# Two model blocks on one core: the conditional overflow part as a loop over groups, splits between MoE and block 2 off GpSimd, and the shared expert's last layer in native fp32

## The chip, the cores and the metric

One core of a Trainium2 chip runs the whole program in one launch. The time is the device time in microseconds; three runs of the kernel before gave a median of 799.4 us (798.35 to 801.41). Engines: TensorE (PE; its weight loads are PEld), VectorE (DVE), ScalarE (ACT), GpSimd (POOL) and SyncE (SP), which here only issues DMAs. A "q" behind an engine's name (PEldq, DVEq) is its sequencer: waits, register work, branches.

## The reference, cut to what matters

256 tokens of width 1024 go through two blocks in fp32. The first has a mixer (attention and convolution) and a MoE; the second has pooling, windowed attention and a gated FFN. The MoE is where the change lies: 32 experts in 4 groups of 8; each token takes one group and two experts of it; beside them one shared expert sees all tokens.

```
g_w, g_idx = lax.top_k(g_prob, 1)                     # one group of 4 per token
e_w, e_idx = lax.top_k(e_prob, TOP_K)                 # two of its 8 experts
hid = jax.nn.silu(a) * b * combine[:, :, None]
routed = jnp.einsum('nef,efd->nd', hid, w_down)
shared = (jax.nn.silu(t @ w_sh_gate) * (t @ w_sh_up)) @ w_sh_down
x = h + rms_norm(routed + shared, post_ffn_norm)      # then the second block
```

## The kernel before

**Weights.** All weights come through one stream (class `Stream`): 167 chunks of 128 x 2048 fp32 (1 MB), each of two granules of 128 x 1024. SP loads chunks into a ring of 7 raw buffers (`RAWB`); a chunk's buffer is free, and the next load is issued, when its second granule has been split. `split` makes of a granule a high part (`whi`, a cast to fp32r on ScalarE, line 116) and a low part (`wlo`, a subtraction, line 119), on VectorE unless `eng`, `W.eng` or `alt` names GpSimd. Both parts have rings of 5 (`RING`). `take` hands out the next granule; `ahead(n)` splits up to n granules beyond the last one taken, `W.n` (4) when no n is given. A product of two such operands (`mm3`, lines 279 to 281) is three single-pass fp32r products: high x high, high x low, low x high.

**Whole granules.** `whole(n)` skips splitting for n chunks and hands out the raw fp32 data; `drop` then frees those chunks and loads the next. Chunks 14 and 15, the shared expert's first layer, are used so: `shared_first` (line 879) multiplies in native fp32.

**The MoE.** Tokens are gathered into one tile of 128 slots for each group by one-hot products. For each of 32 experts TensorE runs the first layer (`gu`), ScalarE and VectorE the gate (`expert_act`), then transposes (`expert_T`), and the last layer into `y`, one expert later. `group_end` splits a group's `y` into `yg`; `scatter` multiplies it by the group's one-hot `sel` and adds it to `ffn[i]`, the sum for token block i (two of 128 tokens). `shared_last` adds the shared expert's last layer to the same sums, from `sTh`/`sTl` (made by `shared_T` early in the MoE) and the granules 222 and 223, which stand in the stream ahead of the last expert's 224 and 225.

**The end of the MoE** (lines 1150 to 1232). `W.n` is set to 2 and `W.eng` to GpSimd. In order of the program: `shared_last(0, (0, 1))`; the last expert's last layer; `W.ahead()`; `group_end(3)`; the scatters of block 0, with one product of the shared layer for each half of block 1 in between (line 1163). Then `many`, the flag that a group has more than 128 tokens, is read into a register of every engine (line 1166), and `tc.If(many > 0)` (line 1167) holds the overflow part: for each of four groups, unrolled, products that gather further tokens, a device loop over 8 experts with their weights loaded anew, and products that add the result. Its products are plain fp32. Behind the `If`: `residual(0)` (norm, residual sum and the next norm's gain, on ScalarE and VectorE), the rest of block 1's sum, and the transposes `half_T` of block 0.

**The start of block 2** (lines 1291 to 1318). Block 0's transposed rows are split into `uTh`/`uTl`, four granules (226 to 229) taken, the queries of block 0 computed (`u_cols`), then `residual(1)`, its transposes, the queries of block 1, `rstd` and `diag` (`dg`, line 368) for both; `W.n` is back at 4, and `W.ahead()` splits 230 to 233, still on GpSimd. The product `spread` (`rs`) needs `dg`; then transposes of the queries (`q2T`), keys and values (`kv`), the pooling inputs (`zp`) and the scores.

**What sets the order.** The program is written against a planner that gives each engine its queue: it follows the order of the program by priority, but lets an instruction that is ready pass one that is not, by its own cost model. Each engine then works through its queue in order. An `If` is a unit: nothing of the outside is moved into it or across it. `tc.issue_after` puts an instruction behind a named one.

Of the kernel before, what the change touches and what calls it, by code (L numbers as in the profile page):

```python
# [11 lines left out]
F32 = mybir.dt.float32  # L12
F32R = mybir.dt.float32r
# [3 lines left out]
ALU = mybir.AluOpType  # L17
# [3 lines left out]
P = 128  # L21
D = 1024
NM = 16
S = 256
# [6 lines left out]
G = 1024  # L31

C_REP, C_MK0, C_MK1, C_LT, C_IOTA, C_REV, C_GB = 0, 128, 272, 544, 672, 1184, 1220
# [5 lines left out]
N_EXP = 32  # L39
CH_EXP = 16  # L40
# [13 lines left out]

ORDER = stream_order()


@with_exitstack
def block_kernel(ctx, tc, rwt, x, meta, pos, wst, gains, cst, pvec, rbias, sink, wpg, cst2, out):
    nc = tc.nc  # L60
    PE, ACT, DVE, POOL = nc.tensor, nc.scalar, nc.vector, nc.gpsimd
# [11 lines left out]
    def split(src, hi, lo, eng=None):  # L73
        ins = ACT.copy(hi, src)
        (eng or DVE).tensor_sub(lo, src, hi.bitcast(F32))
        return ins


    class Stream:
# [26 lines left out]
        def split(self, eng=None, part=None):  # L106

            g, low = self.s, None
            if g != G_HOLE:
                src = self.raw[g // 2][:, (g % 2) * G:(g % 2 + 1) * G]  # L110
                hi = wp.tile([P, G], F32R, name="whi", tag="whi", bufs=RING)
                lo = wp.tile([P, G], F32R, name="wlo", tag="wlo", bufs=RING)
                if self.alt and g % self.alt == 0:
                    eng = POOL
                eng = eng or self.eng or DVE
                ACT.copy(hi, src)  # L116

                def low():
                    eng.tensor_sub(lo, src, hi.bitcast(F32))  # L119

                if not part:
                    low()
                self.parts[g] = (hi, lo)
            self.s += 1
            if g % 2:
                del self.raw[g // 2]
                tag = self.place.get(g // 2)
                if not tag:
                    self.load()
                elif self.again[tag]:  # L130
                    self.again[tag] -= 1
                    self.load(tag)
            return low
# [29 lines left out]
            self.g += 1  # L163
            return self.parts.pop(self.g - 1)

        def whole(self, n):

            if self.s == G_HOLE:
                self.split()
            self.s0 = self.s  # L170
            self.g = self.s = self.s + 2 * n
            return [self.raw[self.g // 2 - n + c][:, a * G:(a + 1) * G] for c in range(n) for a in range(2)]

        def drop(self, n):
            for c in range(n):
                del self.raw[(self.s0 // 2) + c]
                self.load()

    W = Stream()
# [74 lines left out]
    def half_T(src, b, p=P):  # L254

        pt = mmt("tr")
        v = pt[:, :4 * p].rearrange("q (a t) -> q a t", a=4)
        for a in range(4):
            PE.transpose(v[:, a], src[:, (4 * b + a) * P:(4 * b + a + 1) * P], ident[:p, :p])
        return v  # L260
# [23 lines left out]
    def kb(w, k, n=P):  # L284
        return w[:, k * n:(k + 1) * n]
# [6 lines left out]
    def rows(o, w, ah, al, n, first, last):  # L292

        mm3(o, [(ah, al, kb(w[0], n, 512), kb(w[1], n, 512))], first=first, last=last)
# [571 lines left out]
    with tc.tile_pool(name="p2", bufs=1) as p2:  # L866
# [88 lines left out]
        DVE.tensor_scalar(ovf, most, float(P), None, op0=ALU.is_gt)  # L955


        ws = W.whole(2)
        gus = [shared_first(i, ws) for i in range(2)]
        W.drop(2)  # L960
        W.ahead()
        for tag in AGAIN:
            W.load(tag)
# [70 lines left out]
            return hh, hl  # L1034


        sTh = p2.tile([P, 2, S], F32R, name="sTh")
        sTl = p2.tile([P, 2, S], F32R, name="sTl")

        def shared_T(i, hs):  # L1040
            ht = mmt("hT")[:, :256]
            for f in range(2):
                PE.transpose(ht[:, f * P:(f + 1) * P], hs[:, f * P:(f + 1) * P], ident)
            ht = ht.rearrange("p (f t) -> p f t", f=2)
            split(ht, sTh[:, :, i * P:(i + 1) * P], sTl[:, :, i * P:(i + 1) * P])


        def slot_weights():
# [87 lines left out]
        def shared_last(i, ks):  # L1136
            for k in ks:
                for n in range(2):
                    rows(ffn[i][n], wsd[k], sTh[:, k, i * P:(i + 1) * P], sTl[:, k, i * P:(i + 1) * P],
                         n, k == 0, False)  # L1140

        def scatter(i, gs):
            for g in gs:
# [5 lines left out]

        g_pf = gain("post_ffn")  # L1150
        g_m2 = gain("mix2")
        W.n = 2
        W.eng = POOL
        wsd += [W.take(), W.take()]
        shared_last(0, (0, 1))
        last_cols(N_EXP - 1, hid)
# [2 lines left out]
        ffn[1] = [mmt("ffn10"), mmt("ffn11")]  # L1159
        group_end(3)  # L1160
        scatter(0, (0, 1, 2))
        for n in range(2):
            PE.matmul(ffn[1][n], sTh[:, 0, P:], kb(wsd[0][0], n, 512), start=True, stop=False, skip_group_check=True)
        scatter(0, (3,))

        many = nc.values_load(ovf[0:1, 0:1], min_val=0, max_val=1)
        with tc.If(many > 0):
            code2 = r3("code2")
            stt(code2, slot, -float(P) - 65536.0, over, ALU.add, ALU.add)
            ohx = p2.tile([P, 2, P], F32, name="ohx")  # L1170
            sx = p2.tile([P, S], F32, name="sx")
            cwx = p2.tile([P, 9], F32, name="cwx")
            sgx = p2.tile([P, S], F32, name="sgx", tag="sg", bufs=2)
            hx = p2.tile([P, S], F32, name="hx", tag="hs", bufs=2)
            hT = p2.tile([P, S], F32, name="hTx", tag="sg", bufs=2)
            xx, ya = w4("xx"), w4("ya")
            raw = p2.tile([P, 512], F32, name="rawx")
            pa, pb = acct("pa"), acct("pb")
            for g in range(4):
                for i in range(2):  # L1180
                    DVE.tensor_scalar(ohx[:, i], cs[:, C_IOTA + g * P:C_IOTA + (g + 1) * P],
                                      code2[:, i:i + 1], None, op0=ALU.is_equal)
                for b in range(2):
                    for a in range(4):
                        for i in range(2):
                            for src in (th, tl):
                                PE.matmul(kb(pa, a), kb(src[:, i], 4 * b + a).bitcast(F32), ohx[:, i],
                                          start=i == 0 and src is th, stop=i == 1 and src is tl,
                                          skip_group_check=True)
                    DVE.tensor_copy(kb(xx, b, 512), pa)  # L1190
                for i in range(2):
                    PE.matmul(pb[:, :9], ohx[:, i], comb[:, i, g], start=i == 0, stop=i == 1)
                DVE.tensor_copy(cwx, pb[:, :9])
                for i in range(2):
                    PE.transpose(kb(pb, i), ohx[:, i], ident)
                DVE.tensor_copy(sx, pb[:, :S])
                DVE.memset(ya, 0.0)
                with tc.For_i(0, 8, 1) as e:

                    def part(b):  # L1200
                        c = bass.ds(e * 3 + (CH_EXP + 24 * g + b // 4), 1)
                        nc.sync.dma_start(raw, wst[c, :, b % 4 * 512:b % 4 * 512 + 512].rearrange("o p f -> p (o f)"))

                    for k in range(8):
                        part(k)
                        PE.matmul(pa, kb(xx, k), raw, start=k == 0, stop=k == 7)
                    ACT.activation(sgx, pa[:, :256], AF.Silu, scale=cwx[:, 8:9])
                    stt(hx, pa[:, 256:], cwx[:, bass.ds(e, 1)], sgx)
                    for f in range(2):
                        PE.transpose(kb(pb, f), kb(hx, f), ident)  # L1210
                    DVE.tensor_copy(hT, pb[:, :256])
                    for k in range(2):
                        for n in range(2):
                            part(8 + 2 * k + n)
                            PE.matmul(pa, kb(hT, k), raw, start=True, stop=True)
                            DVE.tensor_add(kb(ya, n, 512), kb(ya, n, 512), pa)
                for i in range(2):
                    for n in range(2):
                        PE.matmul(pa, kb(sx, i), kb(ya, n, 512), start=True, stop=True)
                        DVE.tensor_copy(raw, pa)  # L1220
                        DVE.tensor_add(ffn[i][n], ffn[i][n], raw)
        s2 = sm(4)
        nx = [residual(0, ffn[0], g_pf, g_m2, s2)]
        for n in range(2):
            for a, w in ((sTh, wsd[0][1]), (sTl, wsd[0][0])):
                PE.matmul(ffn[1][n], a[:, 0, P:], kb(w, n, 512), start=False, stop=False, skip_group_check=True)
        scatter(1, (0, 2))
        shared_last(1, (1,))
        pts = [half_T(nx[0], 0)]
        scatter(1, (1,))  # L1230
        pts.append(half_T(nx[0], 1))
# [4 lines left out]
    with tc.tile_pool(name="p3", bufs=1) as p3:  # L1236
        uTh = p3.tile([P, 8, S], F32R, name="uTh", tag="th")
        uTl = p3.tile([P, 8, S], F32R, name="uTl", tag="tl")
        with tc.tile_pool(name="p3a", bufs=1) as q3:
# [63 lines left out]
            o_q.append(u_cols("q2", 1, ws, 512))  # L1303
            rn.append(rstd(s2[:, 2:4]))
            dgs.append(diag(rn[1], 0))
            W.n = RING - 1
            W.ahead()
            rs = acct("rs")[:, :S]
            spread(rs, dgs, [(0, P), (P, P)])
            DVE.tensor_copy(R, rs)  # L1310
            W.eng = None
            ws = [W.take() for _ in range(2)]
            for i in range(2):
                queries2(i, o_q[i])
# [487 lines left out]
```

## Time and profile before

| | |
|---|---|
| median of 3 runs | 799.4 us (798.35 to 801.41) |
| profiled execution, device time | 799.25 us |
| its span, first to last instruction | 797.5 us |
| mean granted clock of TensorE | 0.986 |
| busy: PE, DVE, ACT, POOL | 768.4, 613.8, 470.4, 65.1 us |
| DMA | 182.53 MB, mean 229 GB/s |

How to read the rows below. A timeline row gives start, duration (us), engine, line, operation, output<-inputs, shapes and count; in brackets the idle time ahead of it and what ended it. A row of waits gives who waited for whom: total us, times, longest. A row of a line's instructions gives shortest/median/longest duration in ns, then first and last start in us. A row of windows gives the stretch, its length, busy us and instructions of PE, PEld, DVE, ACT and POOL, the granted clock, the DMA share and GB/s. Matmul ends are modelled: each overlaps the start of the next, so the interval between starts is what a matmul costs.

### The profile page before, as it was taken

What the parts mean: (1) busy time and instruction counts of PE and PEld (TensorE: products, weight loads), DVE (VectorE), ACT (ScalarE), POOL (GpSimd) and SP (SyncE); (2) the same over time, 40 slices, a digit from 0 to 9 for tenths busy, and PEclk for the clock granted to TensorE, in tenths of its full rate; (3) what the DMA queues carried; (4) which work ended last, traced back from release to release, by engine and by line L of the source; (5) the groups of instructions that cost most, each with busy time, mean ns of one, the idle gap of its engine ahead of it and who ended that gap; (6) DMA issues with size and microseconds to landing.
All of it is one profiled execution on the core that took longest, in us unless ns stands there. A gap on an engine that the chain in (4) does not pass through costs nothing. (4 is left out here: it accounts for less than half of the span.)

```text
span 797.5 us, 11994 instructions
## 1 busy us (share of the span) xinstructions
PE 768.4 (96%) x4587; PEld 669.7 (84%) x4587; DVE 613.8 (77%) x983; ACT 470.4 (59%) x699; POOL 65.1 (8%) x70
## 2 busy tenths in 40 slices
PE   7989999999999999999999879999999999999996
PEld 5979985788888888888777668999988999999995
DVE  5878678899999989998986769856768566566565
ACT  4646445588788888887777345534556444444442
POOL 5631200000000000000003330000000000000000
PEclk9989999999999999999999999999999999999998
DMA  8736354699889979998998432445445455545101
GB/s 335 302 106 246 112 205 158 229 369 369 310 316 365 366 294 368 373 367 311 361 367 308 163 122 106 144 138 195 159 159 212 164 205 166 204 167 204 54 1 53
DMA packets 27217, 182.53 MB, mean 229 GB/s; under 512 B 3328, under 2 KB 3584, under 8 KB 6160
## 3 DMA queue, kind: packets, MB, share of 16 engines
q1 hardware_dynamic: 25344, 176.96, 59.8%
q0 software_dynamic: 1056, 3.71, 1.4%
q10 hardware_dynamic: 752, 1.01, 0.4%
q8 instruction: 38, 0.62, 0.3%
q14 instruction: 27, 0.22, 0.1%
HBM read 180.62 MB, written 1.05 MB: 228 GB/s over the span
## 5 line engine op out<-in xcount | busy, mean ns | idle before, releaser
L116 ACT CAST whi<-raw 128x1024 fp32r<-128x1024 f32 x328 | 339.8, 1049 | 186.6 <-PE gu L280 49.1
L119 DVE TENSOR_TENSOR wlo<-raw,whi 128x1024 fp32r<-128x1024 f32 x318 | 384.4, 1226 | 83.8 <-ACT whi L116 76.8
L279 PE MATMUL gu<-whi,xg 128*128 128x512 f32 x256 | 102.8, 401 | 0.0
L280 PE MATMUL gu<-wlo,xg 128*128 128x512 f32 x256 | 101.3, 396 | 0.0
L281 PE MATMUL gu<-whi,xg 128*128 128x512 f32 x256 | 100.7, 393 | 0.0
L280 PE MATMUL gu<-u2l,whi 128*128 128x256 f32 x320 | 90.6, 283 | 0.0
L279 PE MATMUL gu<-u2h,whi 128*128 128x256 f32 x320 | 90.6, 283 | 0.0
L281 PE MATMUL gu<-u2h,wlo 128*128 128x256 f32 x320 | 90.6, 283 | 0.0
L280 PEld LDWEIGHTS gu<-u2l,whi 128*128 128x128 f32 x320 | 61.5, 192 | 0.0
L281 PEld LDWEIGHTS gu<-u2h,wlo 128*128 128x128 f32 x320 | 61.4, 192 | 0.0
L279 PEld LDWEIGHTS gu<-u2h,whi 128*128 128x128 f32 x320 | 61.4, 192 | 0.0
L280 PEld LDWEIGHTS gu<-wlo,xg 128*128 128x128 f32 x256 | 48.2, 188 | 11.2 <-DVE wlo L119 1.4
L281 PEld LDWEIGHTS gu<-whi,xg 128*128 128x128 f32 x256 | 48.0, 188 | 10.5
L279 PEld LDWEIGHTS gu<-whi,xg 128*128 128x128 f32 x256 | 48.1, 188 | 9.9
L281 PE MATMUL y<-whi,hl 128*128 128x512 f32 x128 | 50.5, 394 | 0.0
L280 PE MATMUL y<-wlo,hh 128*128 128x512 f32 x128 | 50.5, 394 | 0.0
L119 POOL TENSOR_TENSOR wlo<-raw,whi 128x1024 fp32r<-128x1024 f32 x10 | 24.3, 2443 | 309.8 <-ACT whi L116 309.3
L279 PE MATMUL y<-whi,hh 128*128 128x512 f32 x128 | 48.7, 397 | 0.0
L279 PE MATMUL f<-whi,sh 128*128 128x512 f32 (+1 forms) x110 | 38.2, 349 | 0.0
L280 PE MATMUL f<-wlo,sh 128*128 128x512 f32 (+1 forms) x110 | 38.1, 349 | 0.0
L281 PE MATMUL f<-whi,sl 128*128 128x512 f32 (+1 forms) x110 | 37.8, 348 | 0.0
L279 PE MATMUL gt<-uTh,whi 128*128 128x256 f32 x128 | 36.7, 287 | 0.0
(468 smaller groups left out, 1529.8 us busy)
## 6 DMA issues: line engine op xcount, KB each, us to landing
raw<-in_wst_dram SPq DMA_DIRECT2D x164, 1024.0 KB, 4.8
gain<-in_gains_dram POOLq DMA_DIRECT2D x6, 512.0 KB, 4.3
raw<-in_wst_dram SPq DMA_DIRECT2D x5, 512.0 KB, 8.5
h<-in_x_dram SPq DMA_DIRECT2D x2, 512.0 KB, 4.8
cs<-in_cst_dram SPq DMA_DIRECT2D x1, 612.0 KB, 17.1
out_dram<-mg SPq DMA_DIRECT2D x2, 256.0 KB, 2.6
out_dram<-mg ACTq DMA_DIRECT2D x2, 256.0 KB, 2.8
c<-in_cst_dram POOLq DMA_DIRECT2D x1, 288.0 KB, 3.0
```

The source lines that it names most:

```text
L116: ACT.copy(hi, src)
L119: eng.tensor_sub(lo, src, hi.bitcast(F32))
L279: PE.matmul(o, sh, mh, start=first and i == 0, stop=False, skip_group_check=True)
L280: PE.matmul(o, sh, ml, start=False, stop=False, skip_group_check=True)
L281: last_mm[0] = PE.matmul(o, sl, mh, start=False, stop=last and i == n - 1, skip_group_check=True)
```

## The change

The chunk of the shared expert's last layer joins chunks 14 and 15 in a list `WHOLE`; `split` gives their granules out raw and leaves the buffer with the caller, who frees it by `drop(*chunks)`; `whole` goes. `shared_T` keeps one fp32 copy, and `shared_last` is one native fp32 product where it was three single-pass ones; block 1's first half of it now stands wholly ahead of the `If`, and the four products that completed it behind the `If` go. `W.n = 2` and `W.eng = POOL` go, with their resets. In the overflow part the four unrolled groups become a device loop around the loop over experts.

```diff
+WHOLE = [14, 15, ORDER.index(CH_EXP + 3 * N_EXP)]
...
         def split(self, eng=None, part=None):
             g, low = self.s, None
+            if g // 2 in WHOLE:
+                self.parts[g] = self.raw[g // 2][:, (g % 2) * G:(g % 2 + 1) * G]
+                self.s += 1
+                return low
...
-        def whole(self, n):
...
-        def drop(self, n):
-            for c in range(n):
-                del self.raw[(self.s0 // 2) + c]
+        def drop(self, *chunks):
+            for c in chunks:
+                del self.raw[c]
                 self.load()
...
-        ws = W.whole(2)
+        ws = [W.take() for _ in range(4)]
         gus = [shared_first(i, ws) for i in range(2)]
-        W.drop(2)
+        W.drop(*WHOLE[:2])
...
-            split(ht, sTh[:, :, i * P:(i + 1) * P], sTl[:, :, i * P:(i + 1) * P])
+            ACT.copy(sT[:, :, i * P:(i + 1) * P], ht.rearrange("p (f t) -> p f t", f=2))
...
         def shared_last(i, ks):
             for k in ks:
                 for n in range(2):
-                    rows(ffn[i][n], wsd[k], sTh[:, k, i * P:(i + 1) * P], sTl[:, k, i * P:(i + 1) * P],
-                         n, k == 0, False)
+                    PE.matmul(ffn[i][n], sT[:, k, i * P:(i + 1) * P], kb(wsd[k], n, 512), start=k == 0, stop=False,
+                              skip_group_check=True)
...
-        W.n = 2
-        W.eng = POOL
         wsd += [W.take(), W.take()]
...
-        for n in range(2):
-            PE.matmul(ffn[1][n], sTh[:, 0, P:], kb(wsd[0][0], n, 512), start=True, stop=False, skip_group_check=True)
+        shared_last(1, (0,))
         scatter(0, (3,))
...
-            for g in range(4):
+            with tc.For_i(0, 4, 1) as g:
                 for i in range(2):
...
+                DVE.tensor_scalar(code2, code2, -float(P), None, op0=ALU.add)
...
-                    PE.matmul(pb[:, :9], ohx[:, i], comb[:, i, g], start=i == 0, stop=i == 1)
+                    PE.matmul(pb[:, :9], ohx[:, i], comb[:, i, bass.ds(g, 1)].rearrange("p a b -> p (a b)"),
+                              start=i == 0, stop=i == 1)
...
         nx = [residual(0, ffn[0], g_pf, g_m2, s2)]
-        for n in range(2):
-            for a, w in ((sTh, wsd[0][1]), (sTl, wsd[0][0])):
-                PE.matmul(ffn[1][n], a[:, 0, P:], kb(w, n, 512), start=False, stop=False, skip_group_check=True)
         scatter(1, (0, 2))
         shared_last(1, (1,))
+        W.drop(WHOLE[2])
...
-            W.n = RING - 1
             W.ahead()
...
-            W.eng = None
```

## Rows read from the trace of the kernel before

**Rows 1.** Windows of 20 us from 440 to 500 us.
```profile
440.00:460.00 20.00, 17.88 (x78) 14.23 (x79) 16.01 (x45) 9.30 (x20) 7.76 (x7) 0.91 0.47 152
460.00:480.00 20.00, 15.22 (x100) 14.10 (x98) 13.43 (x14) 7.44 (x11) 7.24 (x7) 0.91 0.34 116
480.00:500.00 20.00, 18.21 (x145) 16.57 (x144) 19.65 (x58) 12.72 (x33) 0.28 (x4) 1.00 0.26 95
```
**Rows 2.** Waits from 425 to 470 us.
```profile
DVE mg L320 <- PEq L1167: 6.4, 1, 6.4
ACT whi L116 <- PE ffn L1226: 5.9, 1, 5.9
...
PE ffn L1226 <- PEq L1167: 4.8, 1, 4.8
PEld rs L374 <- DVE dg L368: 4.7, 1, 4.7
```
**Rows 3.** Instructions of line 1167, the `If`.
```profile
L1167 DVEq COMPARE_BRANCH  x1: 72/72/72, 435.4 to 435.4; - x1
...
L1167 DVEq EVENT_SEMAPHORE  x1: 21/21/21, 436.0 to 436.0; - x1
...
L1167 PEldq COMPARE_BRANCH  x1: 5152/5152/5152, 436.3 to 436.3; - x1
```
**Rows 4.** Timeline from 432 to 450 us: TensorE, ScalarE, VectorE.
```profile
433.42 2.24 PE L1146 MATMUL ffn<-yg,sel 128*128 128x512 f32 x9
...
435.74 1.09 PE L1146 MATMUL ffn<-yg,sel 128*128 128x512 f32 x4
...
437.61 0.20 ACT L205 ACTIVATION_READ_ACCUMULATOR junk<-ffn 128x1 f32 x1
...
442.27 0.15 DVE L248 SCALAR_TENSOR_TENSOR sm<-sm 128x1 f32<-128x1 f32 x1
...
443.74 0.75 DVE L252 SCALAR_TENSOR_TENSOR h<-mg,sm,h 128x512 f32<-128x512 f32 x1
444.52 0.69 DVE L339 TENSOR_TENSOR mg<-h,gain 128x512 f32<-128x512 f32 x1
...
449.89 0.49 PE L279 MATMUL q<-whi,uTh 128*128 128x512 f32 x1
```
**Rows 5.** Timeline from 444 to 468 us: GpSimd and VectorE.
```profile
444.83 2.65 POOL L119 TENSOR_TENSOR wlo<-raw,whi 128x1024 fp32r<-128x1024 f32 x1 [6.52 <-ACT whi L116]
...
445.85 2.18 DVE L252 SCALAR_TENSOR_TENSOR h<-mg,sm,h 128x512 f32<-128x512 f32 x1
...
457.55 0.28 DVE L368 TENSOR_SCALAR dg<-ident,sm 128x128 f32<-128x128 f32 x1
...
460.33 4.89 DVE L252 SCALAR_TENSOR_TENSOR sm<-sm,sm 128x1 f32<-128x1 f32 x3
460.49 7.02 POOL L119 TENSOR_TENSOR wlo<-raw,whi 128x1024 fp32r<-128x1024 f32 x3 [3.35 <-ACT whi L116]
...
465.25 2.42 DVE L368 TENSOR_SCALAR dg<-ident,sm 128x128 f32<-128x128 f32 x1
```
**Rows 6.** Instructions of line 119, the low parts, on VectorE.
```profile
L119 DVE TENSOR_TENSOR wlo<-raw,whi x318: 1205/1225/1795, 14.3 to 777.4; 128x1024 fp32r<-128x1024 f32 x159
```
**Rows 7.** Native fp32 products of `shared_first`: the line's instructions, and eight in the timeline.
```profile
L879 PE MATMUL gus<-raw,tT x32: 592/592/697, 122.6 to 143.5; 128*128 128x512 f32 x32
...
127.03 3.70 PE L879 MATMUL gus<-raw,tT 128*128 128x512 f32 x8 [0.29 <-ACT tT L862]
```
**Rows 8.** Windows behind the two holes of TensorE.
```profile
441.63:449.89 8.26, 8.26 (x34) 6.67 (x35) 7.47 (x15) 3.14 (x5) 3.99 (x2) 0.82 0.19 46
...
467.72:471.89 4.17, 3.91 (x19) 3.75 (x19) 2.56 (x4) 0.00 (x0) 0.00 (x0) 0.59 0.67 251
471.89:480.09 8.20, 8.20 (x68) 7.85 (x66) 3.38 (x5) 3.37 (x6) 0.14 (x2) 1.00 0.11 30
```
**Rows 9.** Timeline of VectorE at the end of the MoE.
```profile
434.02 1.29 DVE L75 TENSOR_TENSOR yg<-y,yg 128x512 fp32r<-128x512 f32 x2 [3.20 <-ACT yg L74]
```

More of the change, by code (lines that the diff above doesn't have):

```diff
@@ L164, in take @@
             return self.parts.pop(self.g - 1)
-        def whole(self, n):
[L168 to L172, printed above, removed]
-        def drop(self, n):
-            for c in range(n):
-                del self.raw[(self.s0 // 2) + c]
+        def drop(self, *chunks):
+            for c in chunks:
+                del self.raw[c]
                 self.load()
@@ L1034, in expert_T @@
             return hh, hl
-        sTh = p2.tile([P, 2, S], F32R, name="sTh")
-        sTl = p2.tile([P, 2, S], F32R, name="sTl")
+        sT = p2.tile([P, 2, S], F32, name="sT")
         def shared_T(i, hs):
@@ L1043, in shared_T @@
                 PE.transpose(ht[:, f * P:(f + 1) * P], hs[:, f * P:(f + 1) * P], ident)
-            ht = ht.rearrange("p (f t) -> p f t", f=2)
-            split(ht, sTh[:, :, i * P:(i + 1) * P], sTl[:, :, i * P:(i + 1) * P])
+            ACT.copy(sT[:, :, i * P:(i + 1) * P], ht.rearrange("p (f t) -> p f t", f=2))
         def slot_weights():
@@ L1178, in block_kernel @@
             pa, pb = acct("pa"), acct("pb")
-            for g in range(4):
+            with tc.For_i(0, 4, 1) as g:
                 for i in range(2):
-                    DVE.tensor_scalar(ohx[:, i], cs[:, C_IOTA + g * P:C_IOTA + (g + 1) * P],
-                                      code2[:, i:i + 1], None, op0=ALU.is_equal)
+                    DVE.tensor_scalar(ohx[:, i], cs[:, C_IOTA:C_IOTA + P], code2[:, i:i + 1], None,
+                                      op0=ALU.is_equal)
+                DVE.tensor_scalar(code2, code2, -float(P), None, op0=ALU.add)
                 for b in range(2):
@@ L1200, in part @@
                     def part(b):
-                        c = bass.ds(e * 3 + (CH_EXP + 24 * g + b // 4), 1)
+                        c = bass.ds(e * 3 + g * 24 + (CH_EXP + b // 4), 1)
                         nc.sync.dma_start(raw, wst[c, :, b % 4 * 512:b % 4 * 512 + 512].rearrange("o p f -> p (o f)"))
```

## The prediction

> **What bounds the kernel now.** I read the stretches of 20 us first. TensorE is busy nearly throughout, and the stretches around the conditional part are where it is not: 17.88, 15.22 and 18.21 of 20 us from 440 to 500 us, with a granted clock of 0.91 in two of them and VectorE at 19.65 in the third [rows 1]. So what happens between the MoE and block 2 is paid for at the end of the kernel; a microsecond gained there is kept as long as nothing later is waiting for another engine.
>
> The table of waits from 425 to 470 us names two holes of TensorE: 4.8 us behind line 1167 (the `If`), and 4.7 us in which `rs` waits for VectorE's `dg` [rows 2]. The events of line 1167 show what the first is: TensorE's compare-and-branch takes 5152 ns, VectorE's 72 ns, and VectorE is 0.6 us later at its next event (435.4 to 436.0) [rows 3]. VectorE's own idle time of 6.4 us ends on TensorE's event behind that branch [rows 2]; it is the same hole seen from the other engine. The overflow body is not executed: no row of its lines exists.
>
> The second hole is made by GpSimd. Three splits on it run from 460.49 for 7.02 us; in that time three [128 x 1] operations of VectorE take 4.89 us together and the 128 x 128 `dg` takes 2.42 us [rows 5]. I take the blocking as the cause because the same happens once more: `h<-mg,sm,h` takes 2.18 us beside the split of 444.83 and 0.75 us at 443.74, without one [rows 4, 5].
>
> **The change part by part.** The sum is made against the profiled execution: span 797.5, device time 799.25, which is 0.15 below the median of 799.4. E is the moment at which TensorE ends its work ahead of the `If`, now 435.74 + 1.09 = 436.83 [rows 4].
>
> *Native fp32.* Ahead of the `If`, 14 single-pass products go (12 of `shared_last(0)` and the two of line 1163) and 6 native ones come (4, and 2 of `shared_last(1, (0,))`). A single-pass product is issued every (2.24 - 1.09)/5 = 0.23 us, by the runs of nine and of four [rows 4]. A native one shows as two records (the 16 calls of line 879 have 32), 0.59 us long, which come every (3.70 - 0.59)/7 = 0.444 us, so 0.89 us a call [rows 7]. 6 x 0.89 - 14 x 0.23 = +2.1 us, all on the path, because TensorE has no gap there. So E moves to 438.9. Bounds: +1.9 (two records of 0.43) to +2.1. Two casts and two subtractions of the shared granules go as well: 2 x 1.22 us of VectorE [rows 6], ahead of time and worth nothing by themselves.
>
> *Four lookahead splits ahead of the `If` on VectorE.* Granules 226 to 229 are now split there, 4 x 1.22 = 4.9 us [rows 6]. Their cover: the 2.4 us just freed and the 3.20 us in which VectorE waits ahead of `yg` at 434.02 [rows 9]. They also no longer wait for ring slots, since 222 and 223 held two of the five until after the `If`. I take 0; without the cover the last split would sit ahead of `yg`: +1.2, still under the 2.76 us of twelve scatter products that TensorE has ahead of group 3's.
>
> *The branch.* By the code, TensorE's body is now four times 54 calls, 50 of them native with two records each: some 104 products and as many weight loads a group, over 800 instructions, and VectorE's four times 21 calls. Afterwards TensorE's is one group and two loops. VectorE's size of body costs 0.6 us, TensorE's 5.2 [rows 3]; the new one (over 208 instructions) lies between and much nearer to the small one. I take 0.6; bounds 0.1 and 5.2. TensorE's sequencer reaches the branch 0.53 us ahead of E (436.3), so 0.2 us of the 4.8 remain.
>
> [...]
>
> *What is late next.* The squares of the residual have run inside the hole: they end 0.98 us after E (437.81) [rows 4], and are now on the path. VectorE's chain then starts at 438.9 + 1.0 = 439.9 instead of 442.27, a shift of 2.4. It takes 3.58 us to the second `h` (442.27 to 445.85) [rows 4, 5], and that takes 0.75 us instead of 2.18, then 0.69 for the last `mg` (as at 444.52): done at 444.9. TensorE: from 439.1, eight scatter products 1.85, two native 1.8, to 442.8; four transposes 0.4 (their `mg` is done at 442.9), eight scatter products 1.85, transposes 0.4: 445.6, and there the queries start. They start at 449.89 now [rows 4]. [...]
>
> *No GpSimd behind the queries.* From 449.89 to the end of the queries nothing but the shift changes. Then `dg`, blocked, is the end of TensorE's wait. Unblocked, all of `rstd` takes 1.47 us (442.27 to 443.74 [rows 4]); its last three operations, which start at 460.33, and `dg` (0.28, as at 457.55 [rows 5]) then end by 461.4 on the old time axis, and TensorE waits from 467.72 - 4.7 = 463.0 on: the wait goes. Second term: **-4.7** [rows 2].
>
> *The clock behind that hole.* From 467.72 to 471.89 the granted clock is 0.59 and 19 products take 4.17 us; at 1.00, from 471.89, 68 take 8.20, 0.12 each [rows 8]. 19 x 0.12 = 2.3: third term **-1.9**.
>
> *The second four splits on VectorE (230 to 233).* 4.9 us, behind `dg` if the planner keeps the order of the program. From `dg` to the first scores VectorE would have some 12.1 us (457.1 to 469.2 on the new time axis) and needs the 2.56 + 3.38 that it does now [rows 8] + 4.9 = 10.8. That is cover with 1.3 us to spare. I count one split (1.2 us) as ending up ahead of a chain operation: **+1.2**; bounds 0 and 4.9.
>
> *Held buffer and the rest.* The raw buffer of the shared chunk is held until behind the `If`; DMA is at 0.34 from 460 to 480 [rows 1] and six buffers remain: 0. Body arithmetic (`code2`, dynamic slice) isn't executed: 0.
>
> Sum: -4.3 - 4.7 - 1.9 + 1.2 = -9.7; 799.25 - 9.7 + 0.15 = **789.7 us**.
>
> **Rivals.** (1) *The branch still waits for its code.* For it: the new body has still over twice the 84 calls of VectorE's. Against it: it is a quarter of the one that waits. Then TensorE restarts at 438.4 + 5.2 = 443.6, has 6.3 us of work to the queries and 1.6 us of slow clock more: 451.5, +1.6 instead of -4.3. 1.6 - 4.7 - 1.9 + 1.2 = -3.8: **795.6**.
>
> (2) *VectorE becomes the bound from the queries to the scores.* For it: 19.65 of 20 us from 480 [rows 1], and a cover of only 1.3. Against it: its blocked time, 8 us [rows 5], goes. All four later splits count: -10.9 + 4.9 = -6.0: **793.4**.
>
> (3) *A split stands in VectorE's queue ahead of a chain operation, its cast still waiting for a ring slot.* VectorE works in order, so `yg`, both residuals and `dg` are then as late as the slot; a cast waits up to 5.9 us for one now [rows 2], harmless while GpSimd takes the result. Price: all eight splits, 9.8, and one such wait, 5.9: -10.9 + 15.7 = +4.8, **804.2**. It decides from 10.9 us on. Against it: two ring slots come free, and a wait of that length needs a slot held across the `If`, which no granule does any more.
>
> **How the numbers follow.** Forecast 0.62 (786.7 to 792), rival 2 0.15, rival 1 0.15, rival 3 0.08. The low end is the sum without the +1.2, and with the 1.8 us that TensorE idles from 480 to 500 [rows 1] given back by an earlier VectorE: 786.7. The high end takes in rival 2 and rival 1, 796. A measurement here can tell about 0.5% from no change: faster is below 795.4, slower above 803.4. Faster: 0.62 + 0.15 + half of rival 1 = 0.84; same 0.09 (the other half, and what of rival 3 stays under 803.4); slower 0.07.
>
> **What would show it.** Right: TensorE's branch under 1 us and a gap there under 1 us; no operation of VectorE between 436 and 470 us beyond its usual length; `rs` right behind the queries; no stretch of low clock in either place; GpSimd without splits after the start. Wrong: a branch of 5 us again (rival 1); TensorE waiting for `wlo`, `qT` or `dg` from VectorE (rival 2); VectorE idle ahead of a split, on ACT's cast (rival 3).

## The result, and the profile after

The changed kernel takes 790.69 us (median of 4 runs, 789.21 to 791.99) beside 800.4 us of the kernel before: ratio 0.9873, 95% interval 0.9848 to 0.9899. The forecast was 789.7 us. Its profiled execution took 790.79 us with a span of 788.8.

Stretches of 20 us (length, busy time and instructions of PE, PEld, DVE, ACT and POOL, granted clock, DMA share, GB/s) answer [rows 1]:

```profile
440.00:460.00 20.00, 17.80 (x82) 13.83 (x83) 16.62 (x51) 9.59 (x23) 2.90 (x7) 1.00 0.51 181
460.00:480.00 20.00, 18.72 (x147) 17.09 (x146) 16.34 (x33) 8.49 (x13) 0.14 (x2) 1.00 0.58 211
480.00:500.00 20.00, 19.49 (x162) 18.80 (x159) 19.77 (x60) 15.75 (x45) 0.28 (x4) 1.00 0.15 54
```

The granted clock is 1.00 in all three, and TensorE's second stretch holds 147 products where it held 100. The events of the `If` (now line 1161) answer [rows 3]: TensorE's branch took 5152 ns and takes 353.

```profile
L1161 PEldq COMPARE_BRANCH  x1: 353/353/353, 436.6 to 436.6; - x1
...
L1161 PEldq EVENT_SEMAPHORE  x1: 51/51/51, 439.8 to 439.8; - x1
```

GpSimd is left with the two splits at the start of the program (instructions of line 125, the low parts):

```profile
L125 POOL TENSOR_TENSOR wlo<-raw,whi x2: 2355/2374/2394, 36.4 to 40.9; 128x1024 fp32r<-128x1024 f32 x2
```

TensorE's timeline after the change, which answers to that part of [rows 4]; the first row is the start of the last expert's transposes, `hT`, and the last one the first product of block 2's scores:

```profile
427.74 0.38 PE L1029 MATMUL hT<-ident,hs 128*128 128x128 f32 x2
...
441.84 1.88 PE L1136 MATMUL ffn<-raw,sT 128*128 128x512 f32 x4
443.15 2.20 PE L1143 MATMUL ffn<-yg,sel 128*128 128x512 f32 x7
445.19 0.60 PE L258 MATMUL tr<-ident,mg 128*128 128x128 f32 x4
445.54 0.48 PE L1143 MATMUL ffn<-yg,sel 128*128 128x512 f32 x1
447.88 0.63 PE L258 MATMUL tr<-ident,mg 128*128 128x128 f32 x4 [1.85 <-DVE mg L338]
448.26 0.48 PE L278 MATMUL q<-whi,uTh 128*128 128x512 f32 x1
...
460.98 0.38 PE L1274 MATMUL q2T<-ident,q2s 128*128 128x128 f32 x2
461.20 0.49 PE L373 MATMUL rs<-dg,ones 128*128 128x128 f32 x2
...
471.41 0.48 PE L1322 MATMUL s2a<-kT,qT 64*128 64x256 f32 x1
```

Of the two holes of [rows 2] nothing is left: `rs` stands behind the queries and two of their transposes without a wait. One wait of 1.85 us is new. I set the two executions against each other by three moments: `hT`, the first product of the queries, and the first product of block 2's scores, S. In the kernel before, the first and the last are these:

```profile
426.68 0.38 PE L1030 MATMUL hT<-ident,hs 128*128 128x128 f32 x2
...
480.10 0.48 PE L1330 MATMUL s2a<-kT,qT 64*128 64x256 f32 x1
```

| | hT | queries start | S | hT to queries | queries to S | hT to S |
|---|---|---|---|---|---|---|
| before | 426.68 | 449.89 | 480.10 | 23.21 | 30.21 | 53.42 |
| after | 427.74 | 448.26 | 471.41 | 20.52 | 23.15 | 43.67 |

So the change is worth 9.75 us between `hT` and S. From S to the end of the span nothing differs (797.5 - 480.10 = 317.40; 788.8 - 471.41 = 317.39). Ahead of `hT` the changed kernel's execution is 1.06 us late, and this is not the change. Three windows from 137.5 to 141.2 us, of before, of after, and of a later execution of the same changed kernel:

```profile
137.50:141.20 3.70, 3.70 (x17) 2.04 (x17) 2.79 (x13) 0.21 (x1) 0.00 (x0) 1.00 0.11 18
```
```profile
137.50:141.20 3.70, 3.70 (x7) 1.65 (x7) 2.78 (x13) 0.21 (x1) 0.00 (x0) 0.54 0.00 0
```
```profile
137.50:141.20 3.70, 3.70 (x15) 1.80 (x14) 3.26 (x19) 0.21 (x1) 0.00 (x0) 1.00 0.33 80
```

At a granted clock of 0.54, 7 records fit where 15 to 17 do at 1.00; ahead of it TensorE ran the same narrow products of `lg` without a pause in all three. In the later execution `hT` is at 425.62 instead of 427.74 and S at 469.30: the same 43.68 us between them, and a span of 786.7.

### The profile page after: what moved, and what is told of

Read it like the earlier page. It is cut to its first block, busy times and chain, and to the rows that moved or that the text cites. A ratio compares the mean times of both kernels' runs of the same rounds, so it can differ in the third digit from the quotient of the medians.

```text
span 788.8 us, 11966 instructions
## 1 busy us (share of the span) xinstructions
PE 766.5 (97%) x4579; PEld 665.4 (84%) x4579; DVE 611.8 (78%) x987; ACT 468.7 (59%) x697; POOL 45.7 (6%) x62
## 5 line engine op out<-in xcount | busy, mean ns | idle before, releaser
L125 DVE TENSOR_TENSOR wlo<-raw,whi 128x1024 fp32r<-128x1024 f32 x324 | 391.4, 1225 | 84.7 <-ACT whi L122 77.5
L280 PE MATMUL gt<-uTh,wlo 128*128 128x256 f32 x128 | 36.3, 283 | 0.0
```

What stands on the lines that cost most here:

```text
L280: last_mm[0] = PE.matmul(o, sl, mh, start=False, stop=last and i == n - 1, skip_group_check=True)
```

## The experiments

All ratios are to the kernel before, run beside each on the same chip (its median was 800.4 to 800.8). Stretches are from one profiled execution of each.

| run | median us | ratio, 95% interval | TensorE's branch | hT to queries | queries to S | hT to S |
|---|---|---|---|---|---|---|
| before | 800.7 | | 5.15 | 23.21 | 30.21 | 53.42 |
| after | 790.69 | 0.9873 (0.9848 to 0.9899) | 0.35 | 20.52 | 23.15 | 43.67 |
| e1, loop alone | 795.68 | 0.9951 (0.9934 to 0.9967) | 0.35 | 20.96 | 29.35 | 50.31 |
| e2, GpSimd alone | 798.12 | 0.9980 (0.9965 to 0.9995) | 5.77 | 27.38 | 24.44 | 51.82 |
| e3, native alone | 803.31 | 1.0027 (1.0009 to 1.0044) | 5.05 | 28.83 | 30.22 | 59.05 |
| e4, after unrolled | 798.34 | 0.9980 (0.9966 to 0.9995) | 6.11 | 29.07 | 23.21 | 52.28 |
| e5, loop and GpSimd | 789.83 | 0.9865 (0.9844 to 0.9886) | 0.35 | 20.09 | 24.71 | 44.80 |
| e6, two groups | 790.93 | 0.9873 (0.9849 to 0.9896) | 4.03 | 21.50 | 23.18 | 44.68 |
| e7, order | 788.78 | 0.9852 (0.9835 to 0.9870) | 0.35 | 19.46 | 23.99 | 43.45 |
| e8, GpSimd reads | 797.16 | 0.9952 (0.9933 to 0.9971) | 0.35 | 20.52 | 30.48 | 51.00 |

**Each part alone.** e1 is before with the loop over groups and nothing else:

```diff
-            for g in range(4):
+            with tc.For_i(0, 4, 1) as g:
...
```

> The kernel before with the loop over groups in the conditional part alone; GpSimd splits and three-product shared layer as before. Theory (two separate holes, each worth its own gap): TensorE's compare-and-branch falls from 5152 ns to about 0.4 us and its gap at the If from 4.8 to about 0.6 us; the queries of block 2 start 3 to 4 us earlier than at 449.89; the gap of 4.7 us ahead of rs and the low clock behind it stay. Time 3 to 4 us under the kernel before, ratio 0.995 to 0.997. Rival A (the gap at the If is the reading of the flag and the drain, not the size of the body): branch and time unchanged, ratio 1.000. Rival B (the gain of the change comes from the If alone, and the gap ahead of rs only moves with it): 8 to 10 us faster, ratio 0.988 to 0.990.

The first theory held: the branch is 0.35 us, the ratio lies in its range, and `rs` still waits, beside GpSimd's splits. The queries start 2.25 us earlier behind `hT`, less than the 3 to 4 expected, because TensorE now waits 1.98 us for `mg`. I take GpSimd's splits, which stay in e1, as the cause of this wait too. TensorE's timeline of e1:

```profile
442.58 0.63 PE L259 MATMUL tr<-ident,mg 128*128 128x128 f32 x4 [1.98 <-DVE mg L339]
...
464.18 0.80 PE L374 MATMUL rs<-dg,ones 128*128 128x128 f32 x2 [4.25 <-DVE dg L368]
```

e2 is before without the GpSimd splits, and so with a lookahead of 4 granules where it was 2:

```diff
-        W.n = 2
-        W.eng = POOL
...
-            W.n = RING - 1
...
-            W.eng = None
```

> The kernel before without GpSimd splits between MoE and block 2 alone (lookahead of 4 on VectorE); unrolled groups and three-product shared layer as before. Theory: no gap ahead of rs, no operation of VectorE beyond its usual length from 440 to 470 us, full clock in keys and values; branch still 5.1 us. Gain 4.7 + 1.9 less up to one split of 1.2: 5.4 to 6.6 us, ratio 0.992 to 0.993. Rival A (VectorE takes over 9.8 us of splits and becomes the bound): gain under 2 us, ratio 0.998 to 1.003, with TensorE waiting for wlo. Rival B (the gap ahead of rs is the wait for the squares, not GpSimd): the gap stays at over 3 us.

The direction was right and the size was not: 0.998 where more was expected. Behind the queries it gains 5.8 us, and ahead of them it loses 4.2. Of the loss 1.3 us are the first hole itself, 6.06 us behind a branch of 5.77 where it was 4.80 behind 5.15; why the branch is longer here no run shows. The other 2.9 lie between the hole and the queries. TensorE, ScalarE and VectorE in e2:

```profile
441.91 0.77 PE L1224 MATMUL ffn<-wlo,sTh 128*128 128x512 f32 x1 [6.06 <-PEq L1165]
```
```profile
443.99 1.04 ACT L116 CAST whi<-raw 128x1024 fp32r<-128x1024 f32 x1 [6.32 <-PE ffn L1224]
```
```profile
445.07 1.23 DVE L119 TENSOR_TENSOR wlo<-raw,whi 128x1024 fp32r<-128x1024 f32 x1 [1.28 <-ACT whi L116]
...
449.20 1.22 DVE L119 TENSOR_TENSOR wlo<-raw,whi 128x1024 fp32r<-128x1024 f32 x1 [0.72 <-ACT whi L116]
```

A cast waits 6.32 us until TensorE has read granules that hold their ring slots across the `If`, and its split stands in VectorE's order between the steps of `residual(0)`. A second one follows at 449.20. That is the third rival's mechanism, in a kernel in which slots are still held there; its price is 2.9 us and not the 15.7 that the rival gave it.

e3 is before with the native last layer alone:

```diff
-                    rows(ffn[i][n], wsd[k], sTh[:, k, i * P:(i + 1) * P], sTl[:, k, i * P:(i + 1) * P],
-                         n, k == 0, False)
+                    PE.matmul(ffn[i][n], sT[:, k, i * P:(i + 1) * P], kb(wsd[k], n, 512), start=k == 0, stop=False,
+                              skip_group_check=True)
...
```

> The kernel before with the shared expert's last layer in native fp32 from unsplit granules alone; GpSimd splits and unrolled groups as before. Theory: TensorE's work from the transposes of the last expert to the If grows by 1.5 to 2.1 us, behind the If four products fewer at the low clock give some of it back; both holes stay: 0 to 2 us slower, ratio 1.000 to 1.0025. Rival (freed ring slots and VectorE time make this edit a gain of its own): 2 us or more faster, ratio 0.9975 or less.

By the median it is 2.6 us slower, just beyond the theory's 2. But its profiled execution (804.45 us, where all twelve lie from 800.3 to 805.3) has 5.6 us more between `hT` and S. The native products account for 1.9 of it; the first hole is 6.74 us long instead of 4.80 (e4 below has the same), and the rest lies behind it, where the first eight products take 3.57 us and those in the kernel before 2.51 (at 443.47). Both holes stand in TensorE's timeline of e3:

```profile
445.01 3.57 PE L1143 MATMUL ffn<-yg,sel 128*128 128x512 f32 x8 [6.74 <-DVE mg L338]
...
472.42 0.80 PE L373 MATMUL rs<-dg,ones 128*128 128x128 f32 x2 [4.48 <-DVE dg L367]
```

**The changed kernel with one part taken back.** e4 unrolls the four groups again (the loop's edit reversed):

```diff
-            with tc.For_i(0, 4, 1) as g:
+            for g in range(4):
...
```

> The changed kernel with the four groups of the conditional part unrolled again. Theory: the branch is 5.1 us again and the gap at the If 4 to 5 us; the squares of the residual run inside it again, so the queries start 3 to 5 us later than in the changed kernel, and the rest follows; 3 to 5 us slower than the changed kernel, ratio to the kernel before 0.992 to 0.994. Rival (the loop matters little once GpSimd is gone, because VectorE's chain behind the If is the bound either way): within 1.5 us of the changed kernel, ratio 0.987 to 0.989.

The direction held, the size was double: 7.7 us over the changed kernel by the medians, 8.6 from `hT` to S. The branch and its event, then TensorE's weight loads (PEld) and products in e4:

```profile
L1161 PEldq COMPARE_BRANCH  x1: 6112/6112/6112, 434.5 to 434.5; - x1
L1161 PEldq EVENT_SEMAPHORE  x1: 51/51/51, 440.7 to 440.7; - x1
```
```profile
440.74 0.19 PEld L1143 LDWEIGHTS ffn<-yg,sel 128*128 128x128 f32 x1 [3.56 <-DVE wlo L125]
444.13 2.85 PEld L1143 LDWEIGHTS ffn<-yg,sel 128*128 128x128 f32 x7 [3.20 <-issue]
```
```profile
444.12 3.57 PE L1143 MATMUL ffn<-yg,sel 128*128 128x512 f32 x8 [6.51 <-DVE h L251]
```

One weight load comes right behind the event, and then there is none for 3.20 us, without a wait that the profile shows. The profile names `h` as the releaser, but `h` had ended 0.5 us before TensorE went on. Instruction fetches tell more: packets of 0.02 MB on DMA queue 8, which the profile lists as `instruction`, two from 436 to 445 us in each of before, e3, e4 and e6. The first one lands 1.4 to 1.5 us before the branch ends (in before at 440.04, the branch at 441.45). In e4 the second lands at 442.77, and TensorE goes on at 444.13, 1.36 us behind it. e3 shows the same: one load at 440.32, a fetch that lands at 443.60, the next load at 445.01, 1.41 us behind. So TensorE's second standstill in e3 and e4 ends like the branch, 1.4 us behind a fetch. In before (442.21 to 443.24) and e6 a second fetch came too, but TensorE had instructions in the meantime; why it had none in e3 and e4, no run shows. Then eight products take 3.57 us, at a granted clock of 0.50.

e5 takes the native products back and keeps loop and GpSimd edit, so it is before with the edits of e1 and e2.

> The kernel before with the loop over groups and without GpSimd splits; the shared expert's last layer as before, three products from split granules. Theory (native fp32 pays for itself because the raw granules leave two ring slots free; with them held across the If, the split of granule 229 stands in VectorE's queue ahead of the residual's chain and waits for its cast, as it did with the GpSimd splits alone removed): branch under 0.5 us, but one or two splits inside the chain of residual(0), so the queries start 2 to 4 us later behind the If than in the changed kernel; 1 to 3 us slower than the changed kernel, ratio to before 0.989 to 0.991. Rival (native fp32 only costs its 1.5 to 2.1 us of TensorE): faster than the changed kernel by 1.5 to 2 us, ratio 0.985.

This missed: the ratio lies under the theory's range, and no difference from the changed kernel can be told in the time. With the branch short, the ring slots come free at once: the cast that waited 6.32 us in e2 starts at 440.10 and waits for nothing (ScalarE in e5). Two splits still stand inside the chain of `residual(0)`, at 441.31 and 444.62, but they cost 1.22 us each and no wait, and TensorE saves the native products' 1.9 us.

```profile
440.10 1.05 ACT L116 CAST whi<-raw 128x1024 fp32r<-128x1024 f32 x1
```

From `hT` to S the profiled execution of e5 is even 1.13 us longer than the changed kernel's. It starts the queries 0.43 us earlier and loses 1.56 behind that, where the clock is low after a wait of 2.21 us for `mg` (window from the start of the queries):

```profile
448.23:452.00 3.77, 3.77 (x13) 2.97 (x12) 3.37 (x16) 0.73 (x3) 0.53 (x1) 0.57 0.73 238
```

So loop and GpSimd edit bring 0.49% and 0.20% alone and 1.35% together, and native fp32 adds nothing measurable to them. Each edit alone leaves a loss that the other takes away: in e1 TensorE still waits 1.98 us for `mg` and 4.25 for `dg`, in e2 the ring slots are still held for the length of the branch.

**How the branch depends on the body.** e6 is the changed kernel with two groups unrolled; groups 2 and 3 of the overflow part are left out (that part isn't executed here).

```diff
-            with tc.For_i(0, 4, 1) as g:
+            for g in range(2):
...
```

> The changed kernel with two groups unrolled in the conditional part instead of the loop over four; the overflow of groups 2 and 3 is left out (the part is not executed with these inputs). TensorE's body is then half of the unrolled one. Theory A (the cost is a step: code that lies beyond what has been fetched ahead costs a full fetch): branch of 5 to 6 us as with four groups, gap of 5 to 7 us, time as with four groups, ratio 0.996 to 0.999. Theory B (the cost grows with the size of the body): branch near 2.5 us, gap of 2 to 3 us, ratio 0.992 to 0.994. Theory C (two groups still lie within it): branch 0.35 us, time as the changed kernel, ratio 0.986 to 0.989.

None of the three came as a whole: the branch takes 4.03 us, nearest to A, but the kernel takes 790.93, the time of C. The branch begins at 437.6, 3.1 us ahead of the end of the products already queued, so TensorE idles only 1.11 us (event, then TensorE's timeline of e6):

```profile
L1161 PEldq COMPARE_BRANCH  x1: 4032/4032/4032, 437.6 to 437.6; - x1
```
```profile
441.83 2.10 PE L1143 MATMUL ffn<-yg,sel 128*128 128x512 f32 x8 [1.11 <-PEq L1161]
```

A body of half the length is neither free nor half the price: 0.35 us for one group's code, 4.03 for two, 5.05 to 6.11 for four. The four kernels with the same body differ by 1.06 us among themselves, so a single run at two groups doesn't show that the price grows with the length; it looks more like a step.

In before, e3, e4 and e6 the branches of 4.03 to 6.11 us end 1.4 to 1.5 us behind a fetch on queue 8. The one of 0.35 us in the changed kernel waits for none: no fetch on that queue lies between 428.46 and 438.44, and the branch ends at 436.99, so I take it that what it jumped to had been there already. Why it wasn't with two groups, no run shows.

**GpSimd and VectorE.** e8 adds three useless subtractions on GpSimd to the changed kernel, behind the second lookahead; they read what is there and write a tile that nobody reads:

```diff
+            jk = w4('jk')
+            for gg in (231, 232, 233):
+                POOL.tensor_sub(jk, W.parts[gg][0].bitcast(F32), W.parts[gg][0].bitcast(F32))
```

> The changed kernel with three useless subtractions on GpSimd added behind the second lookahead (from whi of granules 231 to 233 into a tile that nobody reads), nothing taken off VectorE. Theory (GpSimd's reads block VectorE): VectorE's operations ahead of dg or its splits take 2 us and more instead of 0.15 to 1.2; the wait of rs or of keys and values is 3 to 6 us again and the clock falls behind it; 4 to 7 us slower than the changed kernel, ratio 0.993 to 0.997. Rival (the gap of the kernel before was the planner's order of the splits, not the blocking): VectorE's durations as in the changed kernel, time within 1 us of it, ratio 0.986 to 0.989.

It came as expected, with operations of 1.8 to 1.9 us where I had 2 and more; the second hole is back, in full. GpSimd, VectorE and TensorE in e8:

```profile
456.27 7.69 POOL L1303 TENSOR_TENSOR jk<-whi 128x1024 f32<-128x1024 f32 x3 [3.42 <-ACT whi L122]
```
```profile
L1303 POOL TENSOR_TENSOR jk<-whi x3: 1890/2823/2824, 456.3 to 461.1; 128x1024 f32<-128x1024 f32 x3
```
```profile
456.11 2.06 DVE L251 SCALAR_TENSOR_TENSOR sm<-sm,sm 128x1 f32<-128x1 f32 x2
458.10 1.21 DVE L125 TENSOR_TENSOR wlo<-raw,whi 128x1024 fp32r<-128x1024 f32 x1
459.23 1.84 DVE L251 SCALAR_TENSOR_TENSOR sm<-sm,sm 128x1 f32<-128x1 f32 x1
461.00 1.21 DVE L125 TENSOR_TENSOR wlo<-raw,whi 128x1024 fp32r<-128x1024 f32 x1
462.13 1.91 DVE L367 TENSOR_SCALAR dg<-ident,sm 128x128 f32<-128x128 f32 x1
```
```profile
464.10 0.80 PE L373 MATMUL rs<-dg,ones 128*128 128x128 f32 x2 [4.78 <-DVE dg L367]
```

Nothing waits for the three subtractions, so it is their being there that makes VectorE's small operations long: a [128 x 1] one 1.84 us, and `dg` 1.91 instead of 0.28. VectorE's own splits stay at 1.21 us; beside each of them it is GpSimd's subtraction that grows, from 1.89 to 2.82, and the small operation behind the split ends within 0.1 us of that subtraction (`dg` at 464.04, the last subtraction at 463.96).

**The new wait.** e7 is the changed kernel with `uTl(0)` and `residual(1)` put behind the last `mg` of `residual(0)` in VectorE's order:

```diff
+            mg0 = last[1].ins
+            with tc.issue_after(mg0):
+                transpose_split(nx[0], uTh, uTl, P, 0, pts=pts)
-            transpose_split(nx[0], uTh, uTl, P, 0, pts=pts)
```

> The changed kernel with VectorE's order mended behind the If: the low part uTl of token block 0 and the whole of residual(1) stand behind the last mg of residual(0). In the changed kernel TensorE waits 1.85 us for that mg, because VectorE has uTl ahead of it, and uTl waits for ScalarE. Theory: that wait shrinks to under 0.5 us, the queries start about 1.5 us earlier behind the If, and all of it stays: 1 to 2 us under the changed kernel, ratio to before 0.985 to 0.986. Rival (the queries of block 1 and residual(1) are the bound and absorb it): within 0.5 us of the changed kernel, ratio 0.987 to 0.988.

The wait of 1.85 us goes and the queries start 1.06 us earlier behind `hT`, but by S only 0.2 us of it is left. To see whether the order is worth anything I ran the changed kernel and e7's again on one chip, in five rounds, and with them e5 with e7's order:

> The changed kernel again, in five rounds beside the next two on one chip. Both theories: 790 to 791 us, ratio to before 0.987; the queries start 20 to 21 us behind the last hT and TensorE waits some 1.9 us for VectorE's mg ahead of them.

> The changed kernel with uTl(0) and residual(1) behind the last mg of residual(0) in VectorE's order. Theory L (the 1.85 us in which TensorE waits for mg is what the first term lacked, and a microsecond gained there is kept): 1.0 to 1.5 us under the changed kernel, about 789.3, ratio of the two 0.9985 or less with an interval that leaves out 1. Rival (the wait only changes its place, 0.59 and 0.66 us showing instead, and the stretch is 0.2 us shorter): no difference that five rounds can tell.

> Before with the loop, without the GpSimd splits and with the same order of VectorE, but the shared expert's last layer in three single-pass products. Theory N (native fp32 costs TensorE 1.5 us ahead of the If and saves VectorE about as much behind it; with VectorE's order mended its saving is smaller, its cost the same): 0.5 to 1.5 us under the run with native fp32 and the mended order. Rival (the two keep cancelling): the same time within 0.1%.

The changed kernel took 788.78 us, 0.9864 (0.9836 to 0.9892); with the new order 790.41, 0.9870 (0.9847 to 0.9893); with the new order and single-pass products 790.37, 0.9866 (0.9840 to 0.9893). No order of the three can be told; an interval of a quarter of a per cent leaves out neither the 1 us of theory L nor the 0.5 of theory N. The stretches speak for the rivals: from `hT` to S the changed kernel takes 43.68 us, the new order 43.43, the new order with single-pass products 43.00. The wait changed its place: TensorE in the second run of e7's kernel shows two others, one of them behind the queries' start.

```profile
444.93 0.50 PE L278 MATMUL q<-whi,uTh 128*128 128x512 f32 x1 [0.57 <-DVE uTl L77]
451.76 0.66 PE L258 MATMUL tr<-ident,mg 128*128 128x128 f32 x4 [0.65 <-DVE mg L338]
```

No version beats the changed kernel measurably.

## Why the prediction was right, step by step

The total was right, and the two causes are shown: the loop alone takes away the first hole (e1), its reversal brings it back (e4); GpSimd's splits make the second (e2, e8). The sum of the terms was -9.7 us, and from `hT` to S it measures -9.75. That is luck: the first term fell short by 1.6, and the others brought as much more.

*Native fp32.* E, the end of the last product ahead of the `If`, lies 10.15 us behind `hT` before (436.83) and 12.02 after (439.76): +1.9, the lower bound, where I took +2.1.

*The branch.* 0.35 us where I took 0.6; TensorE idles from 439.76 to 439.91, 0.15 us where I had 0.2. That these agree is luck too: I let the branch begin 0.53 us ahead of E, and it begins 3.1 us ahead of it (436.64), so 0.6 us would have been hidden whole. Rival 1 did not come about. e6 shows how near it was: at two groups the branch already waits 4.03 us. e4 is that rival in this kernel, and it costs 8.6 us where I priced it at 5.9: the branch is in part hidden, but a second standstill of 3.20 us and a granted clock of 0.50 from 444.12 to 447.70 come on top. The 1.6 us of slow clock in that price were an estimate: the 8.26 us at 0.82 of [rows 8] give 1.5, and no run shows the term alone.

*First term, -4.3 forecast (the queries at 445.6 instead of 449.89), -2.7 measured (20.52 against 23.21).* The step that failed is "the last `mg`: done at 444.9". VectorE's chain to the second `h` ran as worked out: it ends at 445.11, 5.35 us behind E, and I had 444.2, 5.3 behind. Then I let `mg` follow at once, as in the kernel before, but it starts 1.94 us later. VectorE in the kernel before, then in the changed kernel:

```profile
448.06 0.69 DVE L339 TENSOR_TENSOR mg<-h,gain 128x512 f32<-128x512 f32 x1
...
448.98 0.69 DVE L75 TENSOR_TENSOR uTl<-tr,uTh 128x512 fp32r<-128x512 f32 x1 [0.23 <-ACT uTh L74]
```
```profile
444.36 0.75 DVE L251 SCALAR_TENSOR_TENSOR h<-mg,sm,h 128x512 f32<-128x512 f32 x1
446.44 0.69 DVE L77 TENSOR_TENSOR uTl<-tr,uTh 128x512 fp32r<-128x512 f32 x1 [1.33 <-ACT uTh L76]
447.05 0.68 DVE L338 TENSOR_TENSOR mg<-h,gain 128x512 f32<-128x512 f32 x1
```

In the planner's new order the two have changed places: `uTl(0)` now stands ahead of `mg` and waits 1.33 us for ScalarE's cast, which waits for TensorE's transposes, which stand behind seven scatter products. So TensorE waits 1.85 us for `mg`, which VectorE's order has delayed. e1 has the order of before; e2 and e3 have the new one, so the GpSimd edit and the native products each bring it alone. Mending it (e7) is worth nothing measurable, because two other waits come in its place.

*Second and third term and the +1.2: -5.4 forecast, -7.06 measured.* `dg` unblocked takes 0.28 us, `rs` doesn't wait (-4.71), and the clock behind it is 1.00: from `rs` to S 10.21 us instead of 12.38 (-2.17, where I had -1.9). The remaining -0.2 lies in the queries. The loss of one split (+1.2) did not come, though two splits do stand ahead of `dg`. VectorE in the changed kernel, the `If` and then the stretch of `dg` [rows 5]:

```profile
438.54 1.22 DVE L125 TENSOR_TENSOR wlo<-raw,whi 128x1024 fp32r<-128x1024 f32 x1 [0.24 <-DVEq L1161]
...
458.53 1.22 DVE L125 TENSOR_TENSOR wlo<-raw,whi 128x1024 fp32r<-128x1024 f32 x1
459.66 0.15 DVE L251 SCALAR_TENSOR_TENSOR sm<-sm,sm 128x1 f32<-128x1 f32 x1
459.73 1.22 DVE L125 TENSOR_TENSOR wlo<-raw,whi 128x1024 fp32r<-128x1024 f32 x1
460.87 0.28 DVE L367 TENSOR_SCALAR dg<-ident,sm 128x128 f32<-128x128 f32 x1
```

The queries and two transposes end on TensorE at 461.2, so `dg` at 461.15 is just in time. The split at 438.54 fell into the time that VectorE waits at the `If` anyway. TensorE's window from there to S:

```profile
461.20:471.41 10.21, 10.21 (x85) 9.82 (x83) 6.80 (x9) 4.97 (x8) 0.14 (x2) 1.00 0.59 221
```

TensorE is busy in all of it: VectorE did not become the bound (rival 2), and with 6.80 us of 10.21 it has 3.4 to spare.

*Rival 3* did not come about in the changed kernel and did in e2. What I gave as the reason against it (no slot is held across the `If` any more) is not the only one: in e5 the granules are held as in e2, and the short branch alone takes the wait away.

*The end.* That a microsecond gained here is kept to the end holds to 0.01 us (317.40 and 317.39 behind S).

## What to carry to other kernels

Look at a branch that is never taken as at code that has to be jumped over: here the jump took 4.03 to 6.11 us over two or four groups, with a code fetch in it, and 0.35 us over one, so a loop in the rarely used body shortened the hot path. In e6 the long jump cost what the products already queued didn't cover, 1.11 of its 4.03 us. Edits around one stall aren't additive: here the lookahead on VectorE was worth little until the branch freed its ring slots, and nearly everything after. And where a stall goes, follow the order of each engine's instructions behind it before you let an operation start "at once": the edit itself can change that order, as it did here for `uTl` and `mg`.

## What the runs showed of the hardware

A short jump takes TensorE 0.35 us and a longer one 4.03 to 6.11 us; in before, e3, e4 and e6 the longer one ends 1.4 to 1.5 us after a fetch of 0.02 MB has landed. In e3 and e4 a second standstill of 4.50 and 3.20 us follows after one weight load, and it ends 1.4 us behind a second fetch. Why TensorE has nothing to do until then in these two and not in before and e6, no run shows.

Beside a GpSimd subtraction of 128 x 1024 a [128 x 1] operation of VectorE takes 1.84 us and a 128 x 128 one 1.91 (e8), where they take 0.15 and 0.28 without (after); a 128 x 512 one takes 2.18 instead of 0.75 (before). A VectorE split of 128 x 1024 stays at 1.21 us, and GpSimd's instruction takes 0.93 us more beside it (e8). Two operations were not lengthened, each with one operand in PSUM: in the kernel before, `mg<-ffn,gain` at 445.13 takes 0.68 us beside the split of 444.83, and `uTl` at 448.98 takes 0.69 beside that of 448.54. Whether that operand is the reason, no run shows.

Two executions of the same program differ by 2.1 us ahead of `hT` with the granted clock at 0.54 or 1.00 from 137.5 to 141.2 us; the six products of `gus` that start there take 4.52 us in one and 2.82 in the other. Why one falls and the other doesn't stays open. Over whole executions the clock goes with the time: the six of the changed kernel in the last comparison took 788.0 to 788.9 us at a mean granted clock of 0.992 to 0.996, and 791.7 and 792.3 us at 0.988 and 0.989.
